# Low parts of the down projection's weights: subtraction on VectorE, or negation on ScalarE and an accumulating DMA

## The chip, the cores and the metric

The kernel runs on one core of one Trainium2 chip. The metric is the device time of one execution in microseconds (us); runs are compared by the median. The core has a matrix engine (TensorE, PE in the profile), VectorE (DVE), ScalarE (ACT), GpSimd (POOL) and SyncE (SP). SP, ACT and POOL issue DMAs, each from a queue of its own that it works off in order; 16 DMA engines carry all of them.

## What is computed

The reference is one inference step of an encoder layer for two groups of tokens that share their weights: 1024 prompt tokens and 32 sample tokens, 1056 in all, with D = 1024. The layer has a gated mixer of windowed attention and a short convolution, a cross-attention into 256 memory tokens, a squared-ReLU MLP with 4096 hidden columns, and a last norm:

```python
def trunk_layer(x, attn_core, conv_left, mem_k, mem_v, g_mix, w_in, conv_w, w_attn_out, w_conv_out,
                w_mix_out, g_cross, w_cq, w_co, g_mlp, w_up, w_down):
...
    x = x + co @ w_co
    hm = rms_norm(x, g_mlp)
    x = x + jnp.square(jax.nn.relu(hm @ w_up)) @ w_down
```

All is float32. Only the last product of the layer, the one with `w_down` (4096 x 1024), is concerned here, and the final norm that follows it.

## The kernel before

**Products in three parts.** TensorE takes its operands as float32r, which is narrower than float32. Every operand is therefore split in a high part (the value cast to float32r) and a low part (the value minus its high part), and a product is three matmuls: high x high, high x low, low x high. In `split` (lines 128 to 130) ScalarE casts and VectorE subtracts; lines 129 and 130 are the names under which the profile lists the two, for weights and for other operands.

**Weights.** Weights come in tiles of 128 x 1024, 512 KB each. The list `worder` holds their order. `fetch_w` (147 to 162) takes a raw tile `wr` and has SP load it (line 159); the pool keeps two such tiles (line 157). `issue_w` (164 to 181) takes a pair of tiles `wh` and `wl` for the two parts, of which there are three pairs each (pool `wp`, line 62; lines 168 and 169), splits the raw tile into them, and appends the pair to `ready`. `next_w` (183) issues weights until three are ready and hands out the first: with `LOOK = 2` a weight is thus prepared two steps of work ahead of its use. A cast into `wh` has to wait until the matmuls of the weight three places earlier have ended; a load into `wr` has to wait until the last reader of the raw tile two places earlier has ended. For some small weights (the dictionary `kept`) the low part is stored in HBM at its first use and loaded again later; none of the weights of this change is among them. In some earlier stages every third raw tile lies in another pool (`third`); from line 1270 on this is off.

**The down projection.** The product is computed by a scheme of seven block products in place of eight, on halves of the tokens, the hidden rows and the output columns. Some of them need sums of blocks of `w_down`; GpSimd makes these early in the kernel (`sum_step`, lines 718 to 741: a load, four additions, a store of 512 KB each, on its own DMA queue) and leaves them in HBM as `wsum_d`. `weight` (132) gives under the key `w_down` a block of the input, and under the key `w_sum` one of these sums.

The stages stand at lines 1894 to 1903, in this order: `b11`, `b21`, `n4` with blocks of `w_down` (24 weights), then `t2`, `n3`, `n1` and `b22` with sums (40 weights, since `b22` is done in two passes, for the first half of the columns and for the second). Each stage has eight steps of one weight each. A step (`part`, lines 1801 to 1811) does 48 matmuls of 264 columns over both banks of 264 columns; in `b22` only one bank is done in a pass, so a step has 24 matmuls and its weight serves for half as long. After the second of the two steps that share a pair of banks, VectorE adds the banks into the residual (line 1793), ScalarE squares what has ended (line 274) and GpSimd sums the squares (line 276) for the last norm.

The other operands, the hidden activations, come from HBM: `pump2` (1619 to 1627) has SP load three tiles of 264 KB per step for the stage that comes next (line 1625) and splits those loaded one step earlier (lines 1319 and 1320). The stages follow the last blocks of the up projection (`up_pair`), whose matmuls are at lines 880 to 882; the first two weights of the down projection are issued inside of the last of these blocks (`worder_go` and the `issue_w` after it).

The program is written as one sequence; the framework sorts each engine's instructions by a simulated timeline, except where an instruction is pinned to the program's order, and adds the waits.

Of the kernel before, what the change touches and what calls it, by code (L numbers as in the profile page):

```python
# [10 lines left out]
F32 = mybir.dt.float32  # L11
F32R = mybir.dt.float32r
AF = mybir.ActivationFunctionType
ALU = mybir.AluOpType
# [26 lines left out]
def hybrid_step(ctx: ExitStack, tc: tile.TileContext, io):  # L41
    nc = tc.nc
    act, dve, pool_e, pe, sp = nc.scalar, nc.vector, nc.gpsimd, nc.tensor, nc.sync
# [3 lines left out]
    def nm(s):  # L47
        uid[0] += 1
        return f"{s}_{uid[0]}"
# [78 lines left out]
    def split(hi, lo, src):  # L128
        act.copy(hi, src)  # L129
        dve.tensor_sub(lo, src, hi.bitcast(F32))  # L130

    def weight(key):
# [8 lines left out]
            src = src[j]  # L141
        return src

    fetched = []
    third = {}

    def fetch_w(raw=None):
        if raw is not None:
            pass
        elif third:  # L150
            third["n"] += 1
        if raw is not None:
            pass
        elif third and third["n"] % 3 == 0:
            raw = third["pool"].tile([P, 4, 256], F32, tag="ws", name=nm("wr3")).rearrange("p q c -> p (q c)")
        else:
            raw = wp.tile([P, 1024], F32, tag="wr", bufs=2, name=nm("wr"))
        src = weight(worder[wpos[0] + len(fetched)])
        load = sp.dma_start(raw.rearrange("p (i c) -> p i c", i=4) if len(src.shape) == 3 else raw, src)
        if third and third["n"] == 3 and third["pool"] is W["pool"]:  # L160
            pin(load)
        fetched.append(raw)

    def issue_w(pieces=(slice(0, 1024),)):
        if not fetched:
            fetch_w()
        raw = fetched.pop(0)
        key = worder[wpos[0]]
        hi = wp.tile([P, 1024], F32R, tag="wh", name=nm("wh"))
        lo = wp.tile([P, 1024], F32R, tag="wl", name=nm("wl"))  # L170
        if kept.get(key) is not None:
            sp.dma_start(lo.bitcast(F32), kept[key])
            act.copy(hi, raw)
        else:
            for at in pieces:
                split(hi[:, at], lo[:, at], raw[:, at])
            if key in kept:
                kept[key] = dram.tile([P, 1024], F32, name=nm("wl_d"))
                sp.dma_start(kept[key], lo.bitcast(F32))
        ready.append((worder[wpos[0]], (hi, lo)))  # L180
        wpos[0] += 1

    def next_w(key):
        while len(ready) <= LOOK and wpos[0] < len(worder) and worder[wpos[0]] is not STOP:
            issue_w()
        k, w = ready.pop(0)
        assert k == key, (k, key)
        return w
# [106 lines left out]
    def norm_x():  # L295
# [45 lines left out]
        with tc.manual_schedule(engines={mybir.EngineType.Activation, mybir.EngineType.DVE}):  # L341
            parts(0, range(1))
            issue_w((slice(0, 256), slice(256, 1024)))
            parts(0, range(1, NF))
            act.copy(ones_r, ones.to_broadcast([P, P]))
            issue_w()
            issue_w()
            squares(0)
# [115 lines left out]
    def do_K(pr, extras=()):  # L464
        def fn(w):
            kt = at_tile([P, NT], F32, "kt")
            ktt[pr] = kt
            for c, (o, n) in enumerate(CH):
                a = acc_tile([P, n])
                gemm(a, w, xg[c])  # L470
                dve.tensor_mul(kt[:, o : o + n], a, R[c])
                after(extras, c)
            sp.dma_start(io["o_k"][pr], kt[:, 896:])

        return fn
# [22 lines left out]
    def do_Q(kv, j, extras=()):  # L498
        def fn(w):
            for c, (o, n) in enumerate(CH):  # L500
                npr = min(n, NPR - o)
                if j == 0:
                    qs[kv, c] = at_tile([P, 4, npr], F32R, "QA" if c < 2 else "QB", 2 if c < 2 else 1)
                    if n > npr:
                        qs[kv, 3] = at_tile([P, 4, n - npr], F32R, "QC")
                a = acc_tile([P, n])
                gemm(a, w, xg[c])
                t = tmp(n)
                dve.scalar_tensor_tensor(t, a, 0.125, R[c], op0=ALU.mult, op1=ALU.mult)
                parts = [(qs[kv, c], slice(0, npr))]  # L510
                if n > npr:
                    parts.append((qs[kv, 3], slice(npr, n)))
                for q, s in parts:
                    for e in range(2):
                        own, other = slice(64 * e, 64 * e + 64), slice(64 - 64 * e, 128 - 64 * e)
                        h = 2 * j + e
                        act.copy(q[own, h], t[own, s])
                        dve.tensor_sub(q[other, h], t[own, s], q[own, h].bitcast(F32))
                after(extras, c)

        return fn
# [156 lines left out]
    def do_gate(to, extras=()):  # L678
        def fn(w):
            for c, (o, n) in enumerate(CH):  # L680
                a = acc_tile([P, n])
                gemm(a, w, xg[c])
                t = gate_slot(c, 0)
                dve.tensor_mul(t, a, R[c])
                act.activation(t, t, AF.Sigmoid)
                to(c, t)
                after(extras, c)

        return fn
# [18 lines left out]
    pieces = [("g", f, q) for f in PAIRS for q in range(2)]  # L708
# [42 lines left out]
    for i, h in enumerate(hosts):  # L751
# [16 lines left out]
        if h[0] == "Q":  # L768
            fn, key = do_Q(h[1], h[2], extras), qt(h[1], h[2])
        elif h[0] == "K":  # L770
            fn, key = do_K(h[1], extras), ("w_in", 8 + h[1])
        elif h[0] == "G":
            fn, key = do_gate(lambda c, t: sa.__setitem__((c, 0), t), extras), ("w_in", 34)
        else:
            fn, key = do_conv(*h, extras), conv_w(h[1], h[0])
# [932 lines left out]
    at = {}  # L1708
# [314 lines left out]
```

## Time and profile before

| what | before |
|---|---|
| runs shown (2) | 1752.73 and 1756.1 us, median 1754.41 us |
| span of the profiled execution, first to last instruction | 1747.8 us |
| what lies around the span, against the median of the runs | 6.6 us |
| busy: TensorE, VectorE, ScalarE, GpSimd | 1727.7, 1188.1, 852.9, 586.2 us |
| mean granted TensorE clock | 0.995 |
| DMA: moved, mean rate | 346.60 MB, 198 GB/s |

The profile gives the profiled execution by its span alone, without a time of its own for the whole run. The profile lists groups of instructions by line, engine and operation, with the tile written and the tiles read (`wl<-wr,wh`), a count, busy time and mean duration. In a timeline each row begins with its start and its duration in us, and ends, in brackets, with the time that the engine was idle before it and what released it. "DMA share" is the mean busy share of the 16 DMA engines in a stretch. The time "to landing" of a DMA counts from its issue to its completion.

### The profile page before, as it was taken

Reading aid. Unit: us, or ns where it says so; the run is one execution under the profiler, and the core shown is the slowest. Engines: PE = TensorE matmul, PEld = TensorE weight load, DVE = VectorE, ACT = ScalarE, POOL = GpSimd, SP = SyncE. Lnnn points to the kernel's source line nnn. Section 1 sums busy time; section 2 is a strip of 40 time slices with the busy share of each in tenths; the row PEclk is TensorE's granted clock in tenths of the full one; section 3 lists DMA queues with packets and bytes.
Section 4 is the critical chain, followed back from the end, with each engine's and each line's share of the span. In section 5 each row is a group of like instructions: output and inputs, shape, how many; then the busy total and the mean of one; then the engine's idle time right before and its main releaser. Section 6 shows DMA issues by size and latency. Waiting matters only on the chain. (4 is left out here: it accounts for less than half of the span.)

```text
span 1747.8 us, 32606 instructions
## 1 busy us (share of the span) xinstructions
PE 1727.7 (99%) x12262; PEld 1712.4 (98%) x12262; DVE 1188.1 (68%) x2276; ACT 852.9 (49%) x1660; POOL 586.2 (34%) x667
## 2 busy tenths in 40 slices
PE   9999999999999999999999999999999999999998
PEld 8999999999999999999999999999999999999998
DVE  7776777768666646555677888787666686545675
ACT  8653534535335324434556666765444463332444
POOL 0026366443553544432224232005555410000121
PEclk9999999999999999999999999999999999999999
DMA  4333344333436888867766667775666695555554
GB/s 185 104 126 128 114 134 153 115 139 127 160 132 204 296 292 280 291 203 238 264 213 198 221 227 241 235 258 191 217 222 219 219 330 185 188 193 169 192 170 160
DMA packets 179854, 346.60 MB, mean 198 GB/s; under 512 B 18657, under 2 KB 101249, under 8 KB 179569
## 3 DMA queue, kind: packets, MB, share of 16 engines
q1 hardware_dynamic: 163504, 290.07, 50.0%
q0 software_dynamic: 15568, 53.68, 8.8%
q8 instruction: 96, 1.57, 0.4%
q10 hardware_dynamic: 624, 0.77, 0.1%
q14 instruction: 62, 0.50, 0.1%
HBM read 250.73 MB, written 93.14 MB: 197 GB/s over the span
## 5 line engine op out<-in xcount | busy, mean ns | idle before, releaser
L129 ACT CAST wh<-wr 128x1024 fp32r<-128x1024 f32 (+1 forms) x214 | 223.8, 1046 | 366.6 <-PE acc L1810 121.4
L130 DVE TENSOR_TENSOR wl<-wr,wh 128x1024 fp32r<-128x1024 f32 (+1 forms) x214 | 275.0, 1285 | 106.2 <-ACT wh L129 105.4
L200 PE MATMUL acc<-X,wh 128*128 128x384 f32 (+1 forms) x864 | 281.5, 326 | 0.0
L201 PE MATMUL acc<-X,wh 128*128 128x384 f32 (+1 forms) x864 | 278.8, 323 | 0.1
L202 PE MATMUL acc<-X,wl 128*128 128x384 f32 (+1 forms) x864 | 277.8, 322 | 0.0
L276 POOL TENSOR_TENSOR xacc<-xacc,ct 128x384 f32<-128x384 f32 (+1 forms) x56 | 75.6, 1354 | 379.9 <-ACT ct L274 378.1
L201 PEld LDWEIGHTS acc<-X,wh 128*128 128x128 f32 x864 | 162.7, 188 | 1.7 <-DVE X L280 0.7
L200 PEld LDWEIGHTS acc<-X,wh 128*128 128x128 f32 x864 | 162.4, 188 | 0.8
L202 PEld LDWEIGHTS acc<-X,wl 128*128 128x128 f32 x864 | 162.4, 188 | 0.1
L200 PE MATMUL acc<-Y,wh 128*128 128x384 f32 (+1 forms) x432 | 139.9, 326 | 3.2 <-DVE ct L1068 2.9
L202 PE MATMUL acc<-Y,wl 128*128 128x384 f32 (+1 forms) x432 | 140.0, 325 | 2.7 <-DMA wl<-wl_d 2.7
L201 PE MATMUL acc<-Y,wh 128*128 128x384 f32 (+1 forms) x432 | 139.7, 324 | 0.0
L129 ACT CAST PTh<-pt 128x512 fp32r<-128x512 f32 (+3 forms) x94 | 45.8, 516 | 112.8 <-PE pt L598 111.4
L1809 PE MATMUL acc<-n,wh 128*128 128x264 f32 x352 | 100.2, 285 | 0.0
L1810 PE MATMUL acc<-n,wh 128*128 128x264 f32 x352 | 100.1, 284 | 0.0
L1811 PE MATMUL acc<-n,wl 128*128 128x264 f32 x352 | 99.9, 284 | 0.0
L735 POOL TENSOR_TENSOR ws<-ws 128x256 f32<-128x256 f32 x100 | 89.5, 895 | 5.6
L735 POOL TENSOR_TENSOR xacc<-xacc 128x256 f32<-128x256 f32 x100 | 86.8, 868 | 5.7 <-DMA xacc<-in_w_in 0.4
L200 PEld LDWEIGHTS acc<-Y,wh 128*128 128x128 f32 x432 | 81.4, 189 | 4.4 <-DVE ct L1068 3.8
L202 PEld LDWEIGHTS acc<-Y,wl 128*128 128x128 f32 x432 | 81.5, 189 | 3.0 <-DMA wl<-wl_d 3.0
L201 PEld LDWEIGHTS acc<-Y,wh 128*128 128x128 f32 x432 | 81.6, 189 | 0.0
L584 ACT ACTIVATE S<-S,nmx 128x257 f32<-128x257 f32 (+1 forms) x132 | 64.2, 488 | 18.9 <-DVE nmx L579 17.6
(432 smaller groups left out, 5554.9 us busy)
## 6 DMA issues: line engine op xcount, KB each, us to landing
wr<-in_w_up SPq DMA_DIRECT2D x53, 512.0 KB, 4.5
wr<-in_w_in SPq DMA_DIRECT2D x52, 512.0 KB, 3.6
wr<-wsum_d SPq DMA_DIRECT2D x40, 512.0 KB, 3.5
wr<-in_w_conv_out SPq DMA_DIRECT2D x24, 512.0 KB, 3.9
wr<-in_w_mix SPq DMA_DIRECT2D x24, 512.0 KB, 5.2
wr<-in_w_down SPq DMA_DIRECT2D x24, 512.0 KB, 3.6
n_d<-Z SPq DMA_DIRECT2D x32, 264.0 KB, 4.2
xacc<-in_w_down POOLq DMA_DIRECT2D x16, 512.0 KB, 4.5
```

The lines of the kernel that those rows point to most:

```text
L129: act.copy(hi, src)
L130: dve.tensor_sub(lo, src, hi.bitcast(F32))
L200: pe.matmul(out, wh[:, a], hi, start=(k == 0), stop=False)
L201: pe.matmul(out, wh[:, a], lo, start=False, stop=False)
L202: pe.matmul(out, wl[:, a], hi, start=False, stop=(k == len(acts) - 1))
L276: pool_e.tensor_tensor(acc, acc, sq, op=ALU.add)
L584: act.activation(stl[:, h, : nk + 1], stl[:, h, : nk + 1], AF.Exp, scale=-1.0, bias=nmx[:, h : h + 1], accum_out=den[:, h : h + 1],)
L735: pin(pool_e.tensor_tensor(t[:, to], t[:, x], t[:, y], op=ALU.add))
L1809: pe.matmul(a, wh[:, s], hi, start=(t == 0 and k == 0), stop=False, skip_group_check=True)
L1810: pe.matmul(a, wh[:, s], lo, start=False, stop=False, skip_group_check=True)
L1811: pe.matmul(a, wl[:, s], hi, start=False, stop=(t == 1 and k == 7), skip_group_check=True)
```

## The change

For weights under the keys `w_down` and `w_sum`, ScalarE casts the raw tile into the high part as before. Then, in place of VectorE's subtraction, ScalarE writes the negated high part into the low part's tile, and GpSimd's queue issues a DMA from SBUF to SBUF that adds the raw tile to it: `lo = -hi + raw`. The low part is then the same difference. All other weights are split as before.

```diff
+    BY_DMA = ("w_down", "w_sum")
     fetched = []
     third = {}
...
         else:
-            for at in pieces:
-                split(hi[:, at], lo[:, at], raw[:, at])
+            if key[0] in BY_DMA:
+                act.copy(hi, raw)
+                act.mul(lo, hi.bitcast(F32), -1.0)
+                pool_e.dma_start(lo, raw, accum_op=ALU.add)
+            else:
+                for at in pieces:
+                    split(hi[:, at], lo[:, at], raw[:, at])
             if key in kept:
```

## The prediction

> **What bounds the kernel now.** I read the page first, then the busy time by stage, then who waits for whom in the last stages, then the casts one by one in order of time, then the DMA issues.
>
> ```profile
> PE 1727.7 (99%) x12262; PEld 1712.4 (98%) x12262; DVE 1188.1 (68%) x2276; ACT 852.9 (49%) x1660; POOL 586.2 (34%) x667
> ```
>
> TensorE is busy for 1727.7 of 1747.8 us. Nothing that shortens VectorE's work can shorten the run unless TensorE waits for it somewhere; so the question is where it waits now and where it will wait. The change touches only the weights of the down projection, from about 1396 us on:
>
> ```profile
> core 0: us, PE busy (x) PEld busy (x) DVE busy (x) ACT busy (x) POOL busy (x), PEclk, DMA share, GB/s
> ...
> 1400.00:1421.00 21.00, 21.00 (x175) 21.00 (x174) 17.13 (x23) 12.26 (x20) 6.70 (x4) 1.00 1.03 367
> ...
> 1470.00:1517.00 47.00, 47.00 (x388) 47.00 (x387) 25.07 (x38) 18.21 (x27) 4.78 (x3) 1.00 0.54 180
> ...
> 1688.00:1735.00 47.00, 47.00 (x388) 47.00 (x388) 26.81 (x46) 20.26 (x29) 10.61 (x7) 1.00 0.53 165
> ```
>
> TensorE has no gap in any of these stretches. VectorE is busy 53% to 82% of them, so what it is relieved of buys nothing: there is no wait to remove. A matmul takes 47/388 = 0.121 us; a double step (48 matmuls, both halves of the columns) lasts 5.85 us, a single step of b22 (24) 2.92 us. There are 64 weights: 48 double steps, then 16 single ones.
>
> How far ahead a weight is made is seen in the casts:
>
> ```profile
> 1552.79 1.05 ACT L129 CAST wh<-wr 128x1024 fp32r<-128x1024 f32 x1 [4.80 <-PE acc L1810]
> 1558.64 1.05 ACT L129 CAST wh<-wr 128x1024 fp32r<-128x1024 f32 x1 [3.20 <-PE acc L1810]
> ```
>
> ```profile
> 1695.67 1.05 ACT L129 CAST wh<-wr 128x1024 fp32r<-128x1024 f32 x1 [3.17 <-DMA wr<-wsum_d]
> ...
> 1701.57 1.05 ACT L129 CAST wh<-wr 128x1024 fp32r<-128x1024 f32 x1 [2.89 <-DMA wr<-wsum_d]
> ```
>
> In the double steps the cast waits for TensorE to release the oldest of three pairs of `wh` and `wl`: 5.85 us apart, the pace of TensorE, two steps (11.7 us) ahead of use. In b22 the casts wait for the *load of the raw weight*. There are two raw buffers, and two weights take 1701.57 - 1695.67 = 5.90 us, just what two single steps need. So b22 already runs on the chain of a raw buffer, with no slack in its rate:
>
> ```profile
> 1698.71 1.23 DVE L130 TENSOR_TENSOR wl<-wr,wh 128x1024 fp32r<-128x1024 f32 x1 [0.73 <-ACT wh L129]
> ```
>
> ```profile
> 1698.00 0.36 SPq L159 DMA_DIRECT2D wr<-wsum_d  x1
> 1699.96 0.36 SPq L159 DMA_DIRECT2D wr<-wsum_d  x1
> ```
>
> The subtraction ends at 1699.94 and the next load into that buffer is issued at 1699.96. Load to cast, 3.6 us (issue at 1698.00, cast at 1701.57); cast 1.05; subtraction 1.23; hand-over 0.1: together 5.98, the 5.90 seen.
>
> **The change, part by part.** *Removed*: 64 subtractions of 1.23 us from VectorE, 79 us, worth nothing by the rows above. *Added on ScalarE*: 64 multiplications over 1024 columns; I price one as the cast, 1.05 us, so 67 us in 340 us where ScalarE is about 40% busy. They hide beside the matmuls, but 1.05 us of each lies in the weight's chain, in place of 1.23. *Added on GpSimd's queue*: 64 accumulating DMAs of 512 KB, from SBUF to SBUF. Both the low part and the raw buffer now wait for the landing. Call X the time from the end of the multiplication to the landing. A raw buffer then turns once in 3.6 + 0.1 + 1.05 + 1.05 + X = 5.8 + X, and in this time two weights pass.
>
> X is not in the trace of before, so I bound it. The nearest rows are GpSimd's own transfers of 512 KB, which are plain:
>
> ```profile
> xacc<-in_w_down POOLq DMA_DIRECT2D x16, 512.0 KB, 4.5
> ws<-in_w_down POOLq DMA_DIRECT2D x16, 512.0 KB, 4.4
> wsum_d<-xacc POOLq DMA_DIRECT2D x16, 512.0 KB, 4.1
> wsum_d<-ws POOLq DMA_DIRECT2D x16, 512.0 KB, 3.8
> ```
>
> ```profile
> DMA to landing us min/median/max: 2.9/4.0/7.4
> ```
>
> ```profile
> DMA to landing us min/median/max: 3.6/4.4/8.1
> ```
>
> The first summary is for the stores, the second for the loads. I take 4.3. The wake-up of GpSimd after ScalarE is 0.14 us (ScalarE ends at 1606.96, GpSimd begins at 1607.10):
>
> ```profile
> 1606.44 0.52 ACT L274 ACTIVATE ct<-Gb 128x384 f32<-128x384 f32 x1
> 1607.10 2.09 POOL L276 TENSOR_TENSOR xacc<-xacc,ct 128x384 f32<-128x384 f32 x1 [103.81 <-ACT ct L274]
> ```
>
> An addition to what lies in the destination has to read the destination too. What one pass of 512 KB costs the 16 engines comes from GpSimd's queue row:
>
> ```profile
> q0 software_dynamic: 15568, 53.68, 8.8%
> ```
>
> 0.088 x 1747.8 = 153.8 us for 53.68 MB is 1.5 us for 0.524 MB. The accumulation costs between nothing more (the read is overlapped) and two more passes, 3.0; I take one, 1.5, the middle. X = 0.2 + 4.3 + 1.5 = 6.0 us; the ends are 0.2 + 2.9 = 3.1 and 0.2 + 8.1 + 3.0 = 11.3.
>
> The Trainium skill, page "Collectives: The Full Stack", section "The bandwidth ceiling: the fold count and why AG ≠ RS ≠ AR", says that the addition inside a DMA costs no cycles but a second source read, and gives 62.28 against 32.35 GB/s; by that factor of 1.93 the surcharge would be 1.4 us and the sum 1 to 3 us lower. No run here shows it yet.
>
> *b22, 16 single steps.* The buffer turns in 5.8 + 6.0 = 11.8 us where TensorE wants two weights in 5.85: 5.95 us lost per pair, over 7.5 pairs (half a pair is in when the stage starts): 45 us. Ends: X = 3.1 gives 3.05 x 6 = 18 us (there the double steps leave more in hand), X = 11.3 gives 84.
>
> *Double steps.* They bear 11.7 us a pair, so X = 5.9 is the point from which they stall; X = 6.0 alone would just reach it. But here the transfers share the engines with the operand loads. Of a step's 5.85 us the engines are taken 0.54, or 3.2 us; an accumulation adds two passes, 3.0. That is 6.2 of 5.85, so they will queue. The price of queueing is bounded by the same load in a free and in a full stretch:
>
> ```profile
> wr<-wsum_d SPq DMA_DIRECT2D x40, 512.0 KB, 3.5
> ```
>
> ```profile
> wr<-in_w_down SPq DMA_DIRECT2D x4, 512.0 KB, 6.1
> ```
>
> The second row is from 1390 to 1425 us, where the engines are full; the difference is 2.6. The pace falls as soon as they queue, which eases it, so I take less than half: 1.0 on X and 0.3 on the load. The turn is 13.1 us, 1.4 over 11.7, over 23 pairs: 32 us. Ends: 0, and (11.3 + 5.8 - 11.7) x 23 = 124.
>
> *Entry.* The first weight has no lead: cast at 1396.46, first use at 1400.6.
>
> ```profile
> 1396.46 1.04 ACT L129 CAST wh<-wr 128x1024 fp32r<-128x1024 f32 x1
> ```
>
> ```profile
> L1809 PE MATMUL acc<-t,wh x128: 280/284/290, 1400.6 to 1731.4; 128*128 128x264 f32 x128
> ```
>
> With two operations of ScalarE and X = 7 its low part lands at 1405.6: 5 us late (ends 1 and 9).
>
> *Queues.* On SP's queue the raw load waits for the accumulation, and the operand loads of the next stage and the stores of y stand behind it; the operands are fetched a stage of 47 us ahead and have room for a few us per step, so nothing is added. On GpSimd's queue the sums of squares (about 2 us each) stand among the DMAs; a rival below prices this.
>
> **Sum.** 45 + 32 + 5 = 82 us on the span of 1747.8 gives 1829.8. The runs' median, 1754.4, lies 6.6 above that span, so the forecast is **1836 us**.
>
> **The rivals.** *A: the accumulation lands like a good plain transfer, and nothing measurable changes.* One mechanism: the read of the destination is overlapped and X stays at about 4.0. Then the double steps hide it (9.8 < 11.7), the entry costs 1, and b22 loses 3.95 over 6.5 pairs, 26 us: 1781. The point from which it decides is X = 5.1, which makes 35 us, 2%. For it: the shortest landings of 2.9 and 3.6. Against: the medians of 3.8 to 4.5 without any addition.
>
> *B: the DMA engines become the bound.* If the accumulation reads and writes in sequence (two more passes), X is 7.5 alone; with 1.0 of queueing in the double steps and 0.3 on the load, a turn there is 14.6: 2.9 x 23 = 67; b22 7.45 x 7.5 = 56; entry 8; together 131 us: 1885. For it: the share of 0.54 plus 4.5 of 5.85 us is over one. Against: the operand loads can move into gaps. The Trainium skill, page "DMA: Bandwidth & Descriptors", section "Issuing engines are not separate DMA queues", says that transfers of all queues interleave on the same 16 engines; the 3.5 against 6.1 us above agrees.
>
> *C: GpSimd's order.* The sums of squares stand ahead of an accumulation in the last stages:
>
> ```profile
> L276 POOL TENSOR_TENSOR xacc<-xacc,ct x20: 805/1562/2097, 1478.3 to 1736.5; 128x384 f32<-128x384 f32 x14, 128x288 f32<-128x288 f32 x6
> ```
>
> If all 20 delayed one by their 1.56 us, 20 x 1.56 / 2 (two buffers share a turn) = 16 us more than the forecast: 1852. Against: most follow the cast by about a microsecond, so that the accumulation is issued behind them only in part.
>
> *D: the change is without effect in time*, because the order of the program shifts so that raw loads come earlier: about 1754. Little speaks for it, since the two raw buffers stay two.
>
> **How the numbers follow.** Forecast 0.52, A 0.15, B 0.20, C 0.10, D 0.03. A measurement of this kernel tells about 2% (35 us) from no change. Faster has no mechanism, 0.02; within 2% is A and most of D, 0.15; slower is the rest, 0.83. The range runs from 1775 (X = 3.5) to 1935 (X = 9 in b22, 10 in the double steps); beyond it lie the far ends of X.
>
> **What would show it.** In the profile after: the subtraction on L130 gone from the `wl` of these 64, 64 multiplications near 1.05 us, 64 DMAs `wl<-wr` on GpSimd's queue landing in about 5.8 us, TensorE waiting in b22 for them, 2 casts per 11.8 us there, and gaps of less than 1 us per double step. The forecast is wrong if landings are under 5 us, if double steps lose more than b22, or if the wait before the casts is not for `wr`.

## The result, and the profile after

| | before | after |
|---|---|---|
| runs, median | 1752.73 and 1756.1, 1754.41 us | 1876.96 and 1878.56, 1877.76 us |
| ratio, 95% interval | | 1.0719 (1.0649 to 1.0788) |
| span of the profiled execution | 1747.8 us | 1876.8 us |
| TensorE busy | 1727.7 us | 1772.2 us |
| TensorE not busy | 20.1 us | 104.6 us |
| double steps, b22 | 287.8, 47.3 us | 353.4, 105.2 us |

The change makes the kernel 123 us slower; 82 us were forecast, in a range to 1935 us. The span grew by 129.0 us: TensorE is not busy for 84.5 us more, and busy for 44.5 us more with the same 12262 matmuls. The span of after lies 1.8 us below the time of its run and that of before 6.6 us below its median, so the profiled execution of before was some 5 us quicker than the runs shown, and the runs' 123 us is the size of the change. The last row counts from the first matmul that reads a low part of the down projection to the first one of b22, and from there to the last one; here and below these stage times are read so.

The head of the page after, and TensorE's longest waits:

```profile
PE 1772.2 (94%) x12262; PEld 1746.9 (93%) x12262; DVE 1114.1 (59%) x2212; ACT 916.7 (49%) x1724; POOL 635.3 (34%) x731
```

```profile
PE acc L1817 <- DMA wl<-wr: 66.4, 27, 5.8
PE acc L1815 <- ACT wh L177: 17.0, 6, 5.6
```

Columns of the second: total us, times, longest. TensorE waits for the accumulations at line 1817 (the product with the low part), and some of the time already for the high part, since the cast is late too. Who holds the cast back stands in ScalarE's waits from 1421 to 1866 us:

```profile
ACT wh L177 <- DMA wr<-wsum_d: 148.9, 25, 9.3
ACT wh L177 <- DMA wr<-in_w_down: 74.3, 13, 9.5
ACT wh L177 <- PE acc L1816: 8.0, 3, 6.3
```

Before, the casts of the double steps waited for TensorE; now nearly all wait for the load of the raw weight, which waits for a raw tile, which waits for the accumulation. This is the turn of the raw tile on which the forecast stood, now in the double steps too. The new DMA by its line and by its queue (1390 us to the end):

```profile
L179 POOL DMA_DIRECT2D wl<-wr x64: 856/866/907, 1399.1 to 1857.2; - x64
...
DMA to landing us min/median/max: 4.5/5.5/9.7
```

```profile
q0 software_dynamic: 9216, 33.56, 38.9%
...
wl<-wr POOLq DMA_DIRECT2D x64, 512.0 KB, 5.5
wr<-wsum_d SPq DMA_DIRECT2D x40, 512.0 KB, 5.0
```

GpSimd needs 0.87 us to issue one (0.53 for a plain one before). 38.9% of 16 engines over 486.8 us, divided by 64, is 2.96 us of all engines per accumulation: two passes of 1.5. The loads beside it land in 5.0 us where they took 3.5. That the raw tile is what holds the load is seen in the order of time: of the 62 raw loads that reuse a tile after an accumulation from it, 55 are issued within 0.1 us of that accumulation's landing. The DMA engines are fuller, and TensorE's clock is lower:

```profile
core 0: us, PE busy (x) PEld busy (x) DVE busy (x) ACT busy (x) POOL busy (x), PEclk, DMA share, GB/s
1421.00:1688.00 267.00, 238.45 (x1807) 234.68 (x1807) 85.40 (x206) 120.26 (x158) 37.22 (x43) 0.94 0.88 227
```

```profile
1761.00:1861.00 100.00, 63.86 (x384) 59.80 (x383) 9.78 (x27) 35.15 (x46) 20.29 (x23) 0.83 0.72 168
```

In b22 the engines are busy 0.72 of the time and TensorE 0.64: neither is full, so a chain of latencies sets the pace. Two casts 13 weights apart give it:

```profile
1766.69 1.04 ACT L177 CAST wh<-wr 128x1024 fp32r<-128x1024 f32 x1 [7.53 <-DMA wr<-wsum_d]
...
1854.42 1.05 ACT L177 CAST wh<-wr 128x1024 fp32r<-128x1024 f32 x1 [7.66 <-DMA wr<-wsum_d]
```

87.7 us for 13 weights is 13.5 us per pair of weights, against 5.90 before and 11.8 forecast.

### The profile page after: what moved, and what is told of

Same layout as the page of the kernel before. It is cut to its first block, busy times and chain, and to the rows that moved or that the text cites. A ratio compares the mean times of both kernels' runs of the same rounds, so it can differ in the third digit from the quotient of the medians.

```text
span 1876.8 us, 32816 instructions
## 1 busy us (share of the span) xinstructions
PE 1772.2 (94%) x12262; PEld 1746.9 (93%) x12262; DVE 1114.1 (59%) x2212; ACT 916.7 (49%) x1724; POOL 635.3 (34%) x731
## 5 line engine op out<-in xcount | busy, mean ns | idle before, releaser
L129 ACT CAST wh<-wr 128x1024 fp32r<-128x1024 f32 (+1 forms) x150 | 156.6, 1044 | 192.3 <-PE acc L207 86.1
L130 DVE TENSOR_TENSOR wl<-wr,wh 128x1024 fp32r<-128x1024 f32 (+1 forms) x150 | 196.8, 1312 | 59.3 <-ACT wh L129 58.6
L177 ACT CAST wh<-wr 128x1024 fp32r<-128x1024 f32 x64 | 67.0, 1047 | 238.8 <-DMA wr<-wsum_d 148.9
L179 POOL DMA_DIRECT2D wl<-wr x64 | 55.6, 868 | 294.4 <-ACT wl L178 257.7
L1817 PE MATMUL acc<-n,wl 128*128 128x264 f32 x352 | 109.1, 310 | 34.0 <-DMA wl<-wr 34.0
L282 POOL TENSOR_TENSOR xacc<-xacc,ct 128x384 f32<-128x384 f32 (+1 forms) x56 | 65.6, 1174 | 172.0 <-ACT ct L280 170.3
L1815 PE MATMUL acc<-n,wh 128*128 128x264 f32 x352 | 107.2, 305 | 5.7 <-ACT wh L177 5.6
L1817 PEld LDWEIGHTS acc<-n,wl 128*128 128x128 f32 x352 | 73.4, 208 | 36.9 <-DMA wl<-wr 36.8
L1816 PE MATMUL acc<-n,wh 128*128 128x264 f32 x352 | 106.5, 303 | 0.0
L741 POOL TENSOR_TENSOR ws<-ws 128x256 f32<-128x256 f32 x100 | 93.9, 939 | 5.9 <-DMA ws<-in_w_up 0.3
L206 PEld LDWEIGHTS acc<-Y,wh 128*128 128x128 f32 x432 | 81.6, 189 | 5.0 <-DVE ct L1074 4.3
```

Of the source, the lines that this page charges most:

```text
L206: pe.matmul(out, wh[:, a], hi, start=(k == 0), stop=False)
L741: pin(pool_e.tensor_tensor(t[:, to], t[:, x], t[:, y], op=ALU.add))
L1815: pe.matmul(a, wh[:, s], hi, start=(t == 0 and k == 0), stop=False, skip_group_check=True)
L1816: pe.matmul(a, wh[:, s], lo, start=False, stop=False, skip_group_check=True)
L1817: pe.matmul(a, wl[:, s], hi, start=False, stop=(t == 1 and k == 7), skip_group_check=True)
```

## The experiments

All times of experiments are single runs, except the pinned one (4 runs), and each is set against runs of the kernel before on its own chip, whose medians were 1745.56 to 1746.94 us; the change, against its own, is +123.3 us. Theory T is the forecast's: the turn of a raw tile sets the pace. E says that only the time on the DMA engines counts. S says that the order on ScalarE and GpSimd delays the low parts.

**The addition left out (e1).**

```diff
-pool_e.dma_start(lo, raw, accum_op=ALU.add)
+pool_e.dma_start(lo, raw)
```

> The DMA copies the raw weight over the low part in place of adding it: the addition is left out, so the low part is the whole raw weight; everything else stands. Theory T (the turn of a raw tile sets the pace: load, two operations of ScalarE, landing; two weights per turn): the landing falls from 5.5 to about 4.0 us and the load from 5.0 to about 4.3, the turn from 13.3 to about 11; double steps are hidden, b22 still loses about 5 us per pair: about 1790 us. Rival E (the DMA engines are full, and only their time counts): the engines need 4.7 of 5.85 us per double step and 3.0 of 2.92 per single step: about 1757 us. Rival S (ScalarE's order and GpSimd's queue delay the low parts): nearly unchanged, 1860 us or more.

Measured 1817.43 us, +71.9. Issue 0.53 us, and the landings:

```profile
DMA to landing us min/median/max: 2.8/4.0/8.1
```

So the addition costs 1.5 us of landing and one pass of the engines, but a plain DMA in this place keeps more than half of the loss. b22 lost 35.7 us, as T has it; the double steps lost 28.6 us, where T and E had none, 16 of them in the first two stages, in the first of which the engines were full before too. From the fifth weight on the casts of the double steps come 12.6 us a pair, where a turn of 11 was expected and 11.7 are free: the loads landed in 4.5 us on average and the copies in 4.7. S fails by 43 us.

**No DMA, the addition on VectorE (e2).**

```diff
-pool_e.dma_start(lo, raw, accum_op=ALU.add)
+dve.tensor_add(lo, lo.bitcast(F32), raw)
```

> The negation stays on ScalarE, VectorE adds the raw weight; no DMA. T: a raw tile turns in 3.6 + 0.1 + 1.05 + 1.07 + 1.23 = 7.05 us against 5.85 wanted in b22, 1.2 us per pair over 7.5 pairs: about 1763 us. E: 1754 us. S: a good part of the loss stays, 1790 us or more.

Measured 1758.1 us, +12.5 where T had 9. b22 takes 56.5 us, 7.06 per pair of weights: the turn of 7.05 that T had added up. The negation by itself costs this little, and 9.2 us of it lie in b22, which has no slack; the other 3 us are no more than what runs of the kernel before differ by (1743.82 to 1748.61 us on one chip).

**A third raw tile (e3).**

```diff
     item(open_down)
+    item(lambda: third.update(n=3, pool=W["pool"]))
```

> As the change, with every third raw weight of the down projection in a tile that lies unused then: three raw tiles in turn. T: three weights pass per turn of 13.3 us, 4.4 us a weight: double steps hidden but for the entry, b22 held by the three low-part tiles at about 3.7 to 4.5 us a step: 1775 to 1800 us. E: the same bytes, the same loss: about 1870 us. S: at most 10 us better than the change.

Measured 1823.52 us, +78.0: 45 us better than the change with the same bytes, so E alone is out; yet 24 us above the top of what T alone gave. What stands in the way is seen in the double steps:

```profile
1421.00:1688.00 267.00, 250.86 (x1962) 249.16 (x1960) 90.59 (x216) 133.02 (x173) 43.00 (x49) 0.95 0.95 252
```

```profile
wl<-wr POOLq DMA_DIRECT2D x63, 512.0 KB, 7.0
```

With the tiles less of a limit the transfers go out closer together, the engines fill to 0.95, and a landing takes 7.0 us. There are two limits, one behind the other. In b22 (1732 to 1805 us) the casts still wait for raw loads, 20.6 of the 24.1 us that they wait.

**The raw tile freed at the cast, first try (e6).**

```diff
-pool_e.dma_start(lo, raw, accum_op=ALU.add)
+pool_e.dma_start(lo.rearrange("p (i c) -> p i c", i=4), weight(key), accum_op=ALU.add)
```

> The accumulating DMA reads the raw weight from HBM once more in place of the raw tile, so that the raw tile is free after the cast; the descriptor ring is 64 bytes larger. The accumulation, its wait and its passes over the engines stay. T: only the load and the cast are left in the turn of a raw tile (6.5 us at most a pair): 1770 to 1800 us, what is left coming from the three low-part tiles in b22 (about 8 + 3 us per three steps). E: as slow as the change or slower, 1870 us or more.

Measured 1903.21 us, +157.7: worse than the change, against T. The weight lies in HBM in rows of 1 KB. GpSimd's timeline:

```profile
1542.99 1.29 POOL L179 DMA_DIRECT2D wl<-in_w_down  x1 [5.65 <-issue]
...
1550.22 1.31 POOL L179 DMA_DIRECT2D wl<-in_w_down  x1 [4.43 <-ACT wh L177]
1558.95 1.29 POOL L179 DMA_DIRECT2D wl<-in_w_down  x1 [7.42 <-ACT n L1325]
```

Issues stand 7.2 and 8.7 us apart, though the negation had ended 6.6 us earlier on average, and a landing takes 7.4. Each of the 63 later issues stands 0.3 to 0.4 us behind the landing of the one before: one transfer at a time. Whether the short rows or the descriptor ring cause this was not tested. So this run replaced one limit by another and did not test T. The next run repeats it with long rows.

**The raw tile freed at the cast, with rows of 4 KB (e10).**

```diff
-pool_e.dma_start(lo, raw, accum_op=ALU.add)
+pool_e.dma_start(lo, io["w_up"][wpos[0] % 32], accum_op=ALU.add)
```

> As the change, but the DMA adds a tile of the up projection's weights from HBM (rows of 4 KB) in place of the raw tile, so the low part holds other numbers; the raw tile is free after the cast, the low part still waits for the landing. T2: the turn of a raw tile no longer binds, the engines' time does: about 1800 to 1825 us, like the third raw tile. T: 1780 us or less. E: 1870 us.

Measured 1796.93 us, +50.4. The wait for the landing stays in full (7.9 us now), and still 73 us of the loss are gone, because the raw tile is not held:

```profile
1421.00:1688.00 267.00, 259.57 (x2099) 258.02 (x2099) 101.35 (x247) 145.20 (x192) 45.33 (x51) 0.99 1.00 270
```

```profile
wl<-in_w_up POOLq DMA_DIRECT2D x53, 512.0 KB, 7.9
```

The DMA engines are full (1.00) and TensorE loses little here: the four inner stages take 47 to 48 us as before, and from 1421 to 1688 us the casts wait for TensorE again (67.4 us, against 27.2 for loads). The double steps bear the bytes; what they did not bear was the turn. b22 takes 73.0 us, 4.56 a step. Two limits come near that, and this run does not tell them apart: the engines' time, 2.8 + 1.5 = 4.3 (45.6% of them over 320 us for 52 transfers' bytes), and the three low-part tiles, which turn in 2.1 + 0.4 + 7.5 + 2.9 = 12.9 us, 4.3 a step.

**The bytes without the waits (e9).**

```diff
-    act.copy(hi, raw)
-    act.mul(lo, hi.bitcast(F32), -1.0)
-    pool_e.dma_start(lo, raw, accum_op=ALU.add)
+    split(hi, lo, raw)
+    pin(pool_e.tensor_copy(seen, hi[:, :1].bitcast(F32)))
+    pin(pool_e.dma_start(spare_d[wpos[0] % 4][:, :1024], io["w_up"][0], accum_op=ALU.add))
```

> Low parts by VectorE as before; after each cast GpSimd issues an accumulating DMA of 512 KB that nobody waits for, from HBM to unused tiles in HBM, tied to the cast by a copy of one column on GpSimd. It holds neither a raw tile nor a low part: the transfers' own time on the engines is all that is added. Theory T2 (two limits: the turn of a raw tile with its waits, and the DMA engines' time): the engines need 6.2 us per double step of 5.85 and 4.5 per single step of 2.92, which makes 17 + 25 us, with the entry about 1800 us. T alone (only the turn counts): 1765 us at most. E alone (only the engines count): as slow as the change, 1870 us.

Measured 1786.94 us, +40.4, between T alone and E alone, 13 us below T2. The engines are as full as they can be, and a raw load takes more than twice as long:

```profile
1421.00:1688.00 267.00, 261.63 (x2118) 260.99 (x2118) 159.58 (x301) 105.81 (x158) 88.95 (x100) 0.99 1.00 279
```

```profile
wr<-wsum_d SPq DMA_DIRECT2D x36, 512.0 KB, 8.0
```

The double steps lose 13 us, b22 30 us. In b22 the bytes act through the turn too, since VectorE's subtraction still holds the raw tile: a load takes 7.2 us there, 7.2 + 0.1 + 1.05 + 1.23 = 9.6 us a pair, and 9.6 were measured (76.9/8). So this run parts the two limits in the double steps alone.

**The waits without the bytes (e11).**

```diff
-pool_e.dma_start(lo, raw, accum_op=ALU.add)
+pool_e.dma_start(lo[:, :128], raw[:, :128], accum_op=ALU.add)
```

> As the change, but the DMA adds only the first 128 of 1024 columns; the rest of the low part stays the negated high part. One eighth of the bytes, the same waits. T2: the turn is 3.6 + 0.1 + 2.1 + 0.4 + a landing of about 3 us = 9.2 us a pair: double steps hidden, b22 loses 3.4 us a pair over 7 pairs, 24 us, and the entry 2: about 1772 us. E: 1750 us.

Measured 1775.41 us, +28.9 (T2: 25). The double steps take 288.4 us, nothing lost; b22 71.6, 8.95 per pair against 9.2 expected.

```profile
wl<-wr POOLq DMA_DIRECT2D x57, 64.0 KB, 2.8
```

```profile
core 0: 1773.6 us, clock 0.995
```

**The small addition with three raw tiles (e12).**

> The small addition of the run before with three raw tiles in turn. T2: neither limit binds in the double steps, in b22 the three low-part tiles turn in 2.1 + 0.4 + 3 + 2.9 = 8.4 us for 8.8 wanted: 1750 to 1756 us. E: 1750 us. If the negation and the order of ScalarE cost something by themselves, it stays here: 1760 us or more.

Measured 1759.81 us, +13.3; the low end of what was named for a cost of ScalarE's own. TensorE still waits 7.1 us for low parts. b22 takes 54.3 us, 3.4 a step, where T2 had 2.9. A raw load takes 3.6 us there and a landing 3.7, so three raw tiles turn in 3.6 + 0.1 + 2.1 + 0.4 + 3.7 = 9.9 us, 3.3 a step: the raw tiles still bind in b22, and the casts there wait 11.8 us for loads and 2.8 for TensorE. The four cases as a square, over the kernel before:

| | two raw tiles | three |
|---|---|---|
| 512 KB added | +123.3 us | +78.0 us |
| 64 KB added | +28.9 us | +13.3 us |

Neither the bytes nor the two tiles alone explain the corner: a long landing costs what it does because it holds one of two tiles.

**One part of the weights alone (e4, e5).** The condition in `issue_w` selects the 16 weights of b22, or the other 48.

> The change for the 16 weights of b22 alone. T: the double steps as before, b22 loses what it loses in the change, about 60 us: about 1812 us. E: the engines need 4.5 us per step of 2.92, 1.6 us over 16 steps: about 1780 us.

> The change for the 48 weights of the double steps alone. T: they lose what they lose in the change, about 68 us with the entry: about 1822 us, and this loss and that of b22 alone add up to the whole, 123 to 129 us. E: the engines need 6.2 us per step of 5.85, 0.35 us over 48 steps: about 1772 us.

Measured 1800.02 us, +53.1, and 1822.22 us, +75.3. The sum, 128.4 us, agrees with the +123.3 of the change (114 to 138 by the interval of its ratio); the two parts lose independently, both nearer to T than to E.

**ScalarE's order held (e7).** Cast and negation pinned to the program's order.

> The change with ScalarE's cast and negation held in the order of the program, so that no other work stands between them that waits for TensorE or VectorE. T: the delays of up to 3.7 us between cast and negation, some 20 us in all over two tiles, go: about 10 us less than the change, 1868 us. S: 1830 us or less.

Measured 1871.07 us (4 runs, 1865.98 to 1880.04), ratio 1.0729 (1.0696 to 1.0761): not to be told from the change's 1.0719. The time between the casts and their negations fell from 27 us in all to 9, and the 10 us that T had for this did not show. S is out as a main cause. Delays like this one do exist in the change, a square that waits for VectorE between the cast at 1781.41 and the negation at 1786.13 of the same weight:

```profile
1781.41 1.03 ACT L177 CAST wh<-wr 128x1024 fp32r<-128x1024 f32 x1
1785.70 0.52 ACT L280 ACTIVATE ct<-Ga 128x384 f32<-128x384 f32 x1 [3.26 <-DVE Ga L1799]
1786.13 1.04 ACT L178 ACTIVATE wl<-wh 128x1024 fp32r<-128x1024 f32 x1
```

**Traffic beside, loosely placed (e8).**

> Low parts by VectorE as before, and 62 accumulating DMAs of 512 KB on GpSimd's queue into a tile that nobody reads, from HBM; they hold neither a raw tile nor a low part. T: only the load gets longer, from 3.6 to about 5 us, which the double steps hide and b22 pays with 1.5 us per pair: about 1765 us. E: most of the change's loss is here: 1840 us or more.

Measured 1858.18 us, +111.2, but it tells nothing about the theories. Nothing tied the accumulations to the weights, and they went out far earlier:

```profile
L179 POOL DMA_DIRECT2D idle<-in_w_up x62: 850/874/924, 1123.5 to 1583.0; - x62
```

From 1123 us on GpSimd forms sums of weights for the up projection, and an accumulation waiting for the one before it held these up. The tied run (e9) took its place.

No version that was tried beats the kernel before, and its stages leave nothing to gain by faster low parts: TensorE did not wait there.

## Why the forecast held, and where its sizes were off

**The cause.** The raw tile's turn was named, and the runs bear it out: b22 follows the turn added up from load, ScalarE, issue and landing in e2 (7.06 against 7.05) and e11 (8.95 against 9.2). Freeing the tile at the cast (e10) takes away most of the loss with the landing still waited for. But one of the forecast's own signs of being wrong came true: the double steps lost more than b22 (65.6 against 57.9 us below; 75.3 against 53.1 as runs of their own), 1.4 us a step where less than 1 was expected. The 123 us measured are half as much again as the 82 of the sum, and the terms below say where.

**X, 6.0 us**, was right in b22: 0.4 from the negation to the issue and 5.4 to the landing on average. In the double steps, where 7.0 was taken, it was 6.1 from the fifth weight on. The one pass more was right too: 2.96 us of the engines against 1.5. The Trainium skill, page "Collectives: The Full Stack", section "The bandwidth ceiling: the fold count and why AG ≠ RS ≠ AR", puts the rate of a collective that copies at 1.93 times that of one that adds, and the reason in the second source read. Here the engines' time is 2.96 against 1.49 us in the run without the addition (22.9% of 16 engines over 410 us for 63 transfers), 1.99, which agrees.

**b22, 45 us forecast, 57.9 measured.** The term that was mis-sized most is the load, kept at 3.6 us; I added queueing in the double steps only. In b22 the load of one tile meets the accumulation of the other. From 1761 to 1861 us:

```profile
wl<-wr POOLq DMA_DIRECT2D x14, 512.0 KB, 5.2
wr<-wsum_d SPq DMA_DIRECT2D x13, 512.0 KB, 4.2
```

These are medians. On average over the twelve weights cast from 1766 us on, a turn is 4.8 from the issue of the load to the cast (3.6 forecast), 2.1 for ScalarE's two operations, 0.6 between them (no term at all), 0.4 + 5.4 to the landing (6.0) and 0.2 to the next load (0.1): 13.5 us against 11.8. The form of the sum held: (13.5 - 5.85) x 7.5 pairs is 57 us.

**Double steps and entry, 37 us forecast, 65.6 measured** between their first low part and b22, besides the 6.3 us by which that first one comes later (5 were forecast). The even 0.7 us per step did not show: the six stages of eight steps take 67, 59, 53, 54, 60 and 60 us, against 53, 47, 47, 47, 47 and 48 before. In the first, where the engines were full before too, 14.6 us are lost. In the five others the turn was 14.0 us a pair (casts from 1434.71 to 1736.33 us, 43 weights) where 13.1 was forecast, 2.3 over the 11.7 that two steps last: 22 pairs make 51 us, and 51 were lost. Here too it is the load: 5.5 us from issue to cast on average, where 3.9 was taken, against 6.1 for X, where 7.0 was; and 0.4 lay between cast and negation. So the queueing was there, but on the load and not on X. In e1 the same row, at 5.0 us, makes the double steps lose where none was expected.

**The clock was no term of the sum.** After a wait the matmuls run at half the pace:

```profile
1760.54 0.59 PE L1817 MATMUL acc<-t,wl 128*128 128x264 f32 x1 [3.63 <-DMA wl<-wr]
1760.93 0.42 PE L1815 MATMUL acc<-t,wh 128*128 128x264 f32 x1
1761.15 0.42 PE L1816 MATMUL acc<-t,wh 128*128 128x264 f32 x1
...
1764.43 0.28 PE L1815 MATMUL acc<-n,wh 128*128 128x264 f32 x1
1764.55 0.28 PE L1816 MATMUL acc<-n,wh 128*128 128x264 f32 x1
```

0.22 us from start to start for three microseconds, then 0.12. The granted clock of the whole run falls from 0.995 to 0.973, which is 41 us of full-speed work, and TensorE's busy time grows by 44.5 us. Little of this lengthened the run. The profile follows back the chain of work that ended last, by line, as a share of the whole span; before and after, as far back as it goes:

```profile
PE acc L1809 6%; PE acc L1810 6%; PE acc L1811 6%; PE acc L880 4%; PE acc L882 4%; PE acc L881 4%; PE pc L880 2%; PE pc L881 2%; PE pc L882 2%; PE pq L231 0%; DMA wr<-in_w_up 0%; DVE wl L130 0%; PE o L1199 0%; PE sc L1163 0%; DVE b L1320 0%
```

```profile
DMA wl<-wr 7%; DMA wr<-wsum_d 6%; PE acc L886 4%; PE acc L888 4%; PE acc L887 4%; DMA wr<-in_w_down 3%; PE pc L886 2%; PE pc L887 2%; PE pc L888 2%; ACT wh L177 1%; ACT wl L178 1%; POOL xacc L282 0%; DMA n<-b_d 0%; ACT n L1325 0%; ACT ct L280 0%
```

Before, the matmuls of the down projection (1809 to 1811) stand first. After, theirs (1815 to 1817) are not in the list, and the accumulation and the raw load have their place: from 1407 us to the end of b22, 459 us, TensorE holds 15 us of the chain. The slower matmuls for the most part filled what would have been a wait. The chain is worked out from who released whom, and no run kept the clock up with waits as long as these, so how much of the 15 us is the clock's own stays open. That the waits grew by 84.5 us and the forecast's sum was 82 is no proof of its terms: it is the 123 us that the sum was to give.

**The rivals.** A fell: the landing is not hidden. B's mechanism, two passes more, fell at 2.96 us; that the engines fill is true, but as the second limit, behind the turn. Its time, 1885 us, lies nearer to the 1877.8 measured than the forecast's 1836, but by luck: its X was 7.5, where 5.8 to 6.1 were measured, and its loads were only 0.3 us longer in the double steps and no longer in b22. C fell: GpSimd issues 0.4 us after the negation in 62 of 64 cases. ScalarE's order delays the negations more, by 27 us over the 64, but e7 took two thirds of that away and was no faster. D fell.

## What to carry to other kernels

Moving work from an idle engine to a DMA lengthens the time for which the DMA's *source* is held, so count the buffers of the source, not only those of the result: here, with two raw tiles, a landing of 5.5 us became a turn of 13 to 14 us for every two weights. Take a buffer's turn apart into rows of the profile, and add to each row what it takes when the other buffer's transfers are in flight. Where an engine at 99% is made to wait, its work after the wait can be slower as well; whether that costs time is read from the chain that ended last, which here hardly went through it.

## What the runs showed of the hardware

An accumulating DMA of 512 KB from SBUF to SBUF took 0.87 us to issue, 4.5 us at least and 5.5 us in the median to land, and 2.96 us of all 16 engines; a plain one 0.53, 2.8, 4.0 and 1.49.

The DMA engines at a share of 1.00 (e9, e10) let the double steps run nearly at full pace: they lost 13 and 18 us, most of it in the first stage and at the end, against 65.6 in the change. In b22, where a weight serves for half as long, the same bytes cost 30 and 26 us.

A wait of 2.59 us was enough for the halved clock:

```profile
1767.79 0.59 PE L1815 MATMUL acc<-t,wh 128*128 128x264 f32 x1 [2.59 <-ACT wh L177]
1768.17 0.42 PE L1816 MATMUL acc<-t,wh 128*128 128x264 f32 x1
```

The Trainium skill, page "TensorE: Matmul & The Clock Gate", section "Part 1: The HAM clock gate (the "warmup" mystery)", has the clock halved after an idle window of about 3.4 us and back after about 3.4 us of work. The granted clock is 0.50 from 1760.43 to 1763.85 us and from 1767.26 to 1770.67, which agrees in length. The idle window does not agree: in the 3.41 us between them TensorE was busy for 1.34, and the wait of 2.59 us is shorter than such a window.

After each of the 16 waits of 2.59 us or more at these matmuls in the run after, the pace fell to half, at once or within nine matmuls; after those of 0.6 to 1.8 us it did not, but for one with a wait of 3.1 us right behind it, and between the two it went both ways. In e11 the stage of b22 is full of waits too, and only the longest, 2.88 us, was followed by the slow pace; the run's clock stays at 0.995.
